# A planner with other costs: PE's durations from the trace, and VectorE kept out of GpSimd's intervals

## The chip, the cores and the metric

The kernel runs on one core of a Trainium2 chip. The metric is the time on the device in microseconds (us). A core has five engines with a queue of instructions each: PE (TensorE, matmuls), DVE (VectorE), ACT (ScalarE), POOL (GpSimd) and SP, which here only issues DMAs. Each engine works its queue in the order in which the program was written, and an instruction whose operands are not ready holds up all that stand behind it. So the time depends on the order in which the instructions of one program are written, also where their set stays the same.

## What is computed

One layer of a hybrid trunk is run for two groups of requests that share the weights: a prompt (16 meta rows and 512 rows) and a sample (64 rows); together 592 rows, of which 576 go on. Cut to its core:

```
h = rms_norm(x, pre_gain)
q,k,v,z,r, sq,sk,sv,sz, mg,ms = split(h @ w_in)        # 2048 -> 11280 columns
log_a = log_sigmoid(r @ w_a2 + b_a) / 16
o_gla = gated linear attention(q, k, v, log_a)         # 4 heads: S = diag(a) S + k v^T, o = q S
y_gla = (rms_norm(o_gla) * silu(z)) @ w_up_gla
o_sb  = stick_breaking_attention(sq, sk, sv)           # 8 heads
y_sb  = (o_sb * silu(sz)) @ w_up_sb
y     = x + rms_norm((sigmoid(mg) * y_gla + sigmoid(ms) * y_sb) @ w_o, post_gain)
```

All data are fp32. Outputs are y, the new keys and values and the GLA state of both groups.

## The kernel before

**Tiles and stages.** Each fp32 product is made of three passes in a reduced format: a weight is split into a high part `whi` (cast by ACT from the raw tile) and the rest `wlo` (raw minus whi, by DVE), the activations likewise into tiles such as `h2h` and `h2l`; PE does hi times hi, hi times lo, lo times hi. A pair of 128-column blocks is multiplied by a Strassen-Winograd scheme: seven products W11, W22, S3, S1, S2, W12, S4 (`ORDERS`), whose weights are the raw quarters or sums of them (`raw<-raw`, DVE). In the projection by w_in each product consists of two units of four k-tiles, 12 matmuls of 288 or 296 columns each, so a pair has 14 units. There are 786 units: 616 in the 44 pairs of the input projection (in order: GLA keys, queries, values and gates; the same for the other heads; the stick-breaking keys, values, queries and gates; the two merge gates), then the up projections, then W_o.

**Streams.** Generators feed the engines: `convert` (ACT, `whi`; it may run four units ahead of PE, since the ring has four buffers), `remain` (DVE, `wlo`), `combine` (DVE, the raw sums), `multiply` (PE). The products' results go through FIFOs (`after`, `follow`): ACT copies a bank to `out` or `u`, and for S2 (`done`, line 488) DVE makes u+bank and u+S1 in place (`u<-u,b`, twice), a sum into `out`, and POOL the last one (`out<-out,u`). A bank that S4 needs comes free only behind the `u` sums, so PE's first unit of S4, two units later, waits for them. A gate's `out` passes through silu (`size`, exp, Ln, subtraction, exp, POOL product; names `e<-out`, `e<-e`, `e<-out,e`, `out<-out,e`) and is then stored. Every store and load is issued on SP's one queue: raw tiles of 512 KB with three buffers, and the tensors that go to DRAM and come back, as d_gk, d_cs.

Beside these runs `background()`: `decays()` (per GLA head two gates, exp, Ln and a scan, written `nu<-reset,tm`, stored to d_cs), then `gla_head` for each of the four heads (`gla_fetch` loads k, cs and q; `gla_level` makes x from cs, exponentiates it on ACT, multiplies by q on DVE and by k on POOL, and PE makes the scores, which DVE copies by a mask, `sc<-lmask,b`), the stick-breaking chains, and the merge.

**What sets the order.** `Plan` writes the program. Each call of an engine goes through `Engine.call`, which tells `Plan.note`; all instructions therefore carry that helper's line, L197 here. `note` gives the instruction a planned start (engine free, operands ready, plus `LATENCY`), and an end by `Plan.cost`. `Plan.run` then resumes the stream whose step is due first:

```
def due(self, e):
    return max(e["ready"] + e["slack"], self.free.get(e["eng"], 0.0)) - self.lead.get(e["name"], 0.0)
```

The planned times reach the chip only as the order on each queue; on the chip an instruction waits for its operands and nothing else. `need` (line 687) also acts on the order alone: a pair's W22 isn't written before the pair two ahead has its first column stored.

Of the kernel before, what the change touches and what calls it, by code (L numbers as in the profile page):

```python
# [9 lines left out]
F32 = mybir.dt.float32  # L10
# [68 lines left out]
class Plan:  # L79


    def __init__(self):
        self.free, self.ready, self.used, self.last, self.streams = {}, {}, {}, 0.0, []
        self.base, self.now = {}, 0.0
        self.quartered, self.psum, self.lead, self.by = set(), set(), {}, {}

    def names(self, x):
# [8 lines left out]
    def at(self, x):  # L96
        return max(self.ready.get(y, 0.0) for y in self.names(x))

    def cost(self, eng, name, out, ins, summed):
        n = 1  # L100
        for x in out.shape[1:]:
            n *= x
        psum = any(x.tensor.name in self.psum for x in ins)
        if eng == "pe":
            dt = ins[0].dtype
            if dt == BF16:
                return 0.107
            if name == "transpose":
                return 0.053 if n < 64 else 0.11
            return max(0.214, n * 1.67e-3) if dt == F32 else max(0.11, n * 0.42e-3) + 0.003  # L110
        if eng == "act":
            return (0.055 if psum else 0.095) + (0.09 if summed or len(ins) > 1 else 0.0) + n * 0.83e-3
        if eng == "dve":
            if name == "tensor_scalar" and not psum:
                return 0.07 + n * 0.52e-3
            return 0.07 + n * (6.3e-3 if name == "reciprocal" else 1.04e-3)
        if name == "memset":
            return 0.04 + n * 0.83e-3
        return 0.15 + n * (3.5e-3 if name == "tensor_scalar" else 2.1e-3)

    def note(self, eng, name, args, kw):
        aps = [x for x in list(args) + list(kw.values()) if isinstance(x, bass.AP)]
        out = kw["out"] if "out" in kw else args[0]
        ins = [x for x in aps if x is not out]
        names = [y for x in ins for y in self.names(x)]
        outs = self.names(out)
        made = outs[1:] or outs
        if "dma" in name:
            size = 4.0
            for x in out.shape:  # L130
                size *= x
            start = max([self.now, self.free.get(eng, 0.0)] + [self.ready.get(x, 0.0) for x in names] + [self.base.get(outs[0], 0.0)])
            self.free[eng] = start + 0.5
            self.free["dma"] = max(self.free.get("dma", 0.0), start + 1.9) + size / 350e3
            end = self.free["dma"] + 1.8
            for x in made:
                self.ready[x] = max(self.ready.get(x, 0.0), end)
            for x in names:
                self.used[x] = max(self.used.get(x, 0.0), end)
            return  # L140
        start = self.free.get(eng, 0.0)
        for x in names + outs:
            by = self.by.get(x)
            if eng != "pe" or by != "pe":
                start = max(start, self.ready.get(x, 0.0) + LATENCY.get((by, eng), 0.1))
        end = start + self.cost(eng, name, out, ins, "accum_out" in kw)
        self.free[eng] = end
        for x in names + outs:
            self.used[x] = max(self.used.get(x, 0.0), end)
        for x in made:  # L150
            self.ready[x] = self.base[x] = end
            self.by[x] = eng
        self.last = end
# [1820 lines left out]
```

## Time and profile before

| | us |
|---|---|
| three runs | 1744.12, 1739.87, 1744.42 |
| their median | 1744.12 |
| the profiled execution, its time | 1741.68 |
| its span, first to last instruction | 1739.9 |
| PE busy | 1670.2 (96% of the span) |
| DVE busy | 1250.6 (72%) |
| ACT busy | 853.8 (49%) |
| POOL busy | 182.2 (10%) |

Matmul times overlap in the pipeline, so PE's busy time is the union of them. Idle time matters where PE has it: the chain that ended last is 89% PE. The views that list what an engine waited for name the instruction that came last before the wait ended. PEclk is TensorE's granted clock as a share of full speed.

### The profile page before, as it was taken

To read this page: it belongs to the slowest core of one execution; us is meant where nothing else is said; L and a number is where in the kernel's file an instruction comes from. 1 tells how busy PE (TensorE), PEld (TensorE's weight loads), DVE (VectorE), ACT (ScalarE), POOL (GpSimd) and SP (SyncE) were. 2 spreads that over 40 slices of the span, in tenths; PEclk is the share of its full clock that TensorE was granted. 3 is DMA by queue.
4 is the path that set the end of the run, shared out by engine and by line. 5 is a ranking of instruction groups with operands and counts; after the bars stand their busy time and mean duration, and the time that the engine had idled before them with its cause. 6 is when DMAs were issued, how large, how long until landed. Compare 5 with 4: busy or idle time off the path is not lost.

```text
span 1739.9 us, 31534 instructions
## 1 busy us (share of the span) xinstructions
PE 1670.2 (96%) x12089; PEld 1610.1 (93%) x12089; DVE 1250.6 (72%) x2081; ACT 853.8 (49%) x1759; POOL 182.2 (10%) x293
## 2 busy tenths in 40 slices
PE   4998999899999999999999999999999999999997
PEld 2798999889999998999999999999999999999996
DVE  5877878887987886886677667666766435687777
ACT  5554444344454353455565555555544323355554
POOL 2100220120130021021020011111000000000000
PEclk9999999999999999999999999999999999999998
DMA  7144234344444424455445544554447444423336
GB/s 189 37 140 131 77 107 139 101 116 123 122 117 128 132 60 119 126 163 159 133 137 152 148 140 117 158 158 126 128 138 218 143 142 124 122 79 103 104 80 218
DMA packets 323904, 224.14 MB, mean 129 GB/s; under 512 B 17436, under 2 KB 293432, under 8 KB 322584
## 3 DMA queue, kind: packets, MB, share of 16 engines
q1 hardware_dynamic: 323016, 219.49, 44.3%
q10 hardware_dynamic: 736, 2.62, 0.4%
q8 instruction: 95, 1.56, 0.4%
q14 instruction: 57, 0.47, 0.1%
HBM read 179.17 MB, written 42.90 MB: 128 GB/s over the span
## 4 chain that ended last, share of the span: by engine, by line
PE 89%; DVE 5%; DMA 2%; ACT 1%; issue 1%; POOL 1%; SPq 0%; DVEq 0%; ACTq 0%; POOLq 0%
PE b L197 89%; DVE wlo L197 2%; DVE raw L197 1%; DMA xt<-in_x_sample 1%; ACT whi L197 0%; DVE u L197 0%; DVE t L197 0%; DMA q<-d_gq 0%; POOL h5l L197 0%; DMA xt<-in_x_prompt 0%; DVE x L197 0%; POOL L L197 0%; DVE out L197 0%; SPq L197 0%; DMA raw<-in_w_in 0%
## 5 line engine op out<-in xcount | busy, mean ns | idle before, releaser
L197 ACT CAST whi<-raw 128x512 fp32r<-128x512 f32 x786 | 482.0, 620 | 627.6 <-PE b L197 516.2
L197 DVE TENSOR_TENSOR wlo<-raw,whi 128x512 fp32r<-128x512 f32 x786 | 552.6, 713 | 303.9 <-ACT whi L197 293.7
L197 DVE TENSOR_TENSOR raw<-raw 128x1024 f32<-128x1024 f32 (+1 forms) x232 | 259.5, 1121 | 6.0
L197 PE MATMUL b<-m,whi 128*128 128x288 f32 x912 | 183.5, 296 | 0.0
L197 PEld LDWEIGHTS b<-m,whi 128*128 128x128 f32 x912 | 146.1, 188 | 0.0
L197 PE MATMUL b<-h0h,whi 128*128 128x288 f32 (+1 forms) x480 | 134.3, 304 | 1.3 <-ACT whi L197 1.3
L197 PE MATMUL b<-m,wlo 128*128 128x288 f32 x456 | 134.2, 294 | 0.0
L197 PE MATMUL b<-h6h,whi 128*128 128x288 f32 (+1 forms) x480 | 133.8, 303 | 0.0
L197 PE MATMUL b<-h6l,whi 128*128 128x288 f32 (+1 forms) x480 | 131.5, 298 | 1.9 <-DVE h6l L197 1.8
L197 PE MATMUL b<-h4h,whi 128*128 128x288 f32 (+1 forms) x480 | 133.0, 302 | 0.0
L197 PE MATMUL b<-h1h,whi 128*128 128x288 f32 (+1 forms) x480 | 132.1, 300 | 0.0
L197 PE MATMUL b<-h0l,whi 128*128 128x288 f32 (+1 forms) x480 | 131.5, 299 | 0.0
L197 PE MATMUL b<-h4l,whi 128*128 128x288 f32 (+1 forms) x480 | 130.4, 296 | 0.0
L197 PE MATMUL b<-h1l,whi 128*128 128x288 f32 (+1 forms) x480 | 130.3, 296 | 0.0
L197 PE MATMUL b<-h0h,wlo 128*128 128x288 f32 (+1 forms) x416 | 124.4, 299 | 1.5 <-DVE wlo L197 1.5
L197 PE MATMUL b<-h4h,wlo 128*128 128x288 f32 (+1 forms) x416 | 123.2, 296 | 1.6 <-DVE wlo L197 1.6
L197 PE MATMUL b<-h1h,wlo 128*128 128x288 f32 (+1 forms) x416 | 123.3, 296 | 0.8 <-DVE wlo L197 0.8
L197 PE MATMUL b<-h6h,wlo 128*128 128x288 f32 (+1 forms) x416 | 123.7, 297 | 0.0
L197 PE MATMUL b<-h2h,whi 128*128 128x288 f32 (+1 forms) x352 | 112.5, 319 | 10.7 <-DVE u L197 10.7
L197 PE MATMUL b<-h2h,wlo 128*128 128x288 f32 (+1 forms) x352 | 107.5, 305 | 1.0 <-DVE wlo L197 1.0
L197 PE MATMUL b<-h5h,whi 128*128 128x288 f32 (+1 forms) x352 | 108.5, 308 | 0.0
L197 PE MATMUL b<-h3h,whi 128*128 128x288 f32 (+1 forms) x352 | 107.9, 307 | 0.0
(263 smaller groups left out, 4084.8 us busy)
## 6 DMA issues: line engine op xcount, KB each, us to landing
raw<-in_w_in SPq DMA_DIRECT2D x176, 512.0 KB, 4.5
raw<-in_w_o SPq DMA_DIRECT2D x32, 512.0 KB, 4.0
raw<-in_w_up_gla SPq DMA_DIRECT2D x16, 512.0 KB, 5.3
raw<-in_w_up_sb SPq DMA_DIRECT2D x16, 512.0 KB, 4.7
d_mg<-out SPq DMA_DIRECT2D x16, 288.0 KB, 2.2
d_ms<-out SPq DMA_DIRECT2D x16, 288.0 KB, 2.1
gate<-d_mg SPq DMA_DIRECT2D x16, 288.0 KB, 5.4
gate<-d_ms SPq DMA_DIRECT2D x16, 288.0 KB, 5.5
```

The costliest lines, as they stand in the source:

```text
L197: return real(*args, **kw)
```

## The change

In `Plan.cost`, five of PE's durations and one of DVE's change: a bf16 matmul is planned with 0.056 us instead of 0.107, a transpose with 0.11 whatever its size, an fp32 matmul with 0.224 at least instead of 0.214, and the reduced-format matmul of 288 columns with 0.1325 us (288 x 0.4167e-3 + 0.0125) instead of 0.124; a `scalar_tensor_tensor` with more than two inputs on DVE with 0.125 instead of 0.07 at its base.

In `Plan.note`, the planned intervals of POOL's operations and of those DVE operations that read two SBUF operands of the output's shape (`shared`: wlo, raw sums, `x<-x,q`, `e<-out,e`, `out<-u,b` where both lie in SBUF, ...) are kept in two lists, and each of either kind is planned to start behind any interval of the other kind that it would overlap. Only planned times change by this, not what is written.

```
+        self.port = {"pool": [], "dve": []}
...
+    def shared(self, out, ins):
+
+        n = [x for x in ins if x.tensor.name not in self.psum and x.shape[1:] == out.shape[1:]]
+        return len(n) > 1
...
-                return 0.107
+                return 0.056
             if name == "transpose":
-                return 0.053 if n < 64 else 0.11
-            return max(0.214, n * 1.67e-3) if dt == F32 else max(0.11, n * 0.42e-3) + 0.003
+                return 0.11
+            return max(0.224, n * 1.67e-3 + 4e-3) if dt == F32 else max(0.112, n * 0.4167e-3 + 0.0125)
...
+            if name == "scalar_tensor_tensor" and len(ins) > 2:
+                return 0.125 + n * 1.04e-3
...
-        end = start + self.cost(eng, name, out, ins, "accum_out" in kw)
+        took = self.cost(eng, name, out, ins, "accum_out" in kw)
+        if name != "memset" and (eng == "pool" or eng == "dve" and self.shared(out, ins)):
+            for t0, t1 in sorted(self.port["pool" if eng == "dve" else "dve"]):
+                if t0 < start + took and t1 > start:
+                    start = t1
+            self.port[eng] = self.port[eng][-23:] + [(start, start + took)]
+        end = start + took
```

Both kernels have the same instructions on every engine (PE 11541, DVE 2073, ACT 1677, SP 640 by the program); their order differs from the first pair on. The changed kernel's helper line is L211. Three places follow in which the order moves.

**DVE around the two `u` sums of S2.** For S2 of pair 18 (pairs counted from 0) before:

```order
L197 TENSOR_TENSOR raw<-raw 128x1024
L197 TENSOR_TENSOR x_6435<-x_6435,q 128x10x32
L197 TENSOR_TENSOR wlo<-raw,whi 128x512 x4
L197 TENSOR_TENSOR raw<-raw 128x1024 x2
L197 TENSOR_TENSOR out<-out,b_6375 128x288
L197 TENSOR_TENSOR u<-u,b_6458 128x288
L197 TENSOR_TENSOR u<-u,b_6418 128x288
L197 TENSOR_TENSOR out<-u,b_6375 128x288
```

For S2 of pair 21 now:

```order
L211 TENSOR_TENSOR raw<-raw 128x1024
L211 TENSOR_TENSOR x_7330<-x_7330,q 128x4x64
L211 TENSOR_TENSOR x_7333<-x_7333,q 128x40x8
L211 TENSOR_TENSOR raw<-raw 128x1024
L211 TENSOR_TENSOR x_7376<-cs 128x20x16 x2
L211 TENSOR_TENSOR u<-u,b_7278 128x296
L211 TENSOR_TENSOR u<-u,b_7228 128x296
L211 TENSOR_TENSOR out<-u,b_7177 128x8
L211 TENSOR_TENSOR out<-u,b_7177 128x288
```

The sums `u<-u,b` stand ahead of the wlo of the third unit behind S2 in both; before, this happens in pairs 4, 8 and 18, now in pairs 10, 16 and 21, and in the places shown six instructions stand between a wlo and the sums now, where three stood before.

**SP, the loads with which the first GLA head starts.** k, cs and q are loaded from DRAM; d_cs is the store of a scan, d_gz that of a gate, raw a weight tile (two loads each). Before:

```order
L197 DMA d_cs_1635<-nu 128x640
L197 DMA lmask<-in_consts 128x512
L197 DMA raw<-in_w_in 128x8x128 x2
L197 DMA k<-d_gk_907 128x528
L197 DMA k<-d_gk_907 128x64
L197 DMA cs<-d_cs_1007 128x640
L197 DMA q<-d_gq_1227 128x512
L197 DMA q<-d_gq_1227 128x64
```

Now:

```order
L211 DMA d_gv_2057<-out 128x592
L211 DMA d_cs_2067<-nu 128x640
L211 DMA lmask<-in_consts 128x512
L211 DMA d_gz_1783<-out 128x576
L211 DMA k<-d_gk_965 128x528
L211 DMA k<-d_gk_965 128x64
L211 DMA cs<-d_cs_1063 128x640
L211 DMA q<-d_gq_1231 128x512
L211 DMA q<-d_gq_1231 128x64
L211 DMA raw<-in_w_in 128x8x128 x8
```

The loads moved from behind two raw loads to behind the gate's store d_gz_1783 (and behind the last scan's d_cs), with eight raw loads now behind them.

**ACT at the end of pair 6 and the start of pair 7, where `whi` of units 92 to 101 stands (a pair has 14 units).** The rows with e are two gates' silu, those with x the head's levels. Before:

```order
L197 ACTIVATE e<-e 128x288
L197 CAST whi<-raw 128x512 x3
L197 ACTIVATE e<-e 128x288
L197 ACTIVATE e<-e,one 128x288
L197 COPY x_2643<-b_2605 128x496
L197 COPY x_2643<-b_2555 128x16
L197 COPY x_2643<-b_2606 128x64
L197 ACTIVATE e<-e 128x288
L197 CAST whi<-raw 128x512 x5
L197 COPY x_2775<-b_2737 128x496
```

Now, where two silu chains and two levels stand ahead of `whi` of unit 98:

```order
L211 CAST whi<-raw 128x512 x2
L211 ACTIVATE e<-e 128x288
L211 ACTIVATE e<-e,one 128x288
L211 ACTIVATE e<-e 128x288
L211 ACTIVATE x_2587<-x_2587 128x640
L211 COPY out<-b_2338 128x8
L211 COPY out<-b_2338 128x288
L211 ACTIVATE e<-e 128x288
L211 ACTIVATE e<-e,one 128x288
L211 ACTIVATE x_2657<-x_2657 128x640
L211 ACTIVATE e<-e 128x288
L211 CAST whi<-raw 128x512 x4
```

The two chains, which stood apart by several `whi` before, now stand in one block with the exponentials of two levels.

## Rows read from the trace of the kernel before

**Rows 1.** The page's head and its first part: busy time of each engine, share of the span, instructions.

```profile
span 1739.9 us, 31534 instructions
PE 1670.2 (96%) x12089; PEld 1610.1 (93%) x12089; DVE 1250.6 (72%) x2081; ACT 853.8 (49%) x1759; POOL 182.2 (10%) x293
```

**Rows 2.** Busy time by stage: the stretch in us from the span's start, its length, then PE, PEld, DVE, ACT, POOL with their instructions, PEclk, DMA share, GB/s. The three stretches are the GLA heads, the stick-breaking chains with the merge gates, and the up and W_o projections.

```profile
50.00:700.00 650.00, 616.76 (x4418) 595.56 (x4417) 520.91 (x863) 307.78 (x615) 97.78 (x133) 0.97 0.39 111
700.00:1340.00 640.00, 637.61 (x4672) 614.99 (x4671) 440.61 (x671) 347.76 (x673) 69.00 (x145) 1.00 0.51 146
1340.00:1739.00 399.00, 390.97 (x2903) 384.72 (x2902) 257.55 (x466) 170.45 (x403) 2.90 (x1) 0.99 0.43 125
```

**Rows 3.** What PE waited for from 50 to 700 us: total us, times, longest.

```profile
PE b L197 <- DVE u L197: 10.7, 3, 4.2
PE b L197 <- DVE cs L197: 5.8, 4, 2.7
PE b L197 <- DMA q<-d_gq: 5.5, 1, 5.5
PE b L197 <- DVE wlo L197: 4.9, 6, 1.6
PE b L197 <- DMA x<-d_gv: 2.7, 2, 1.4
```

**Rows 4.** The same columns as rows 2 for short stretches after a wait (two of seven), and for PE alone in a stretch without waits.

```profile
316.00:326.00 10.00, 5.78 (x30) 5.62 (x29) 8.93 (x17) 2.16 (x5) 2.48 (x4) 0.66 0.49 137
604.00:612.00 8.00, 6.49 (x30) 6.52 (x31) 5.89 (x15) 3.02 (x5) 2.35 (x3) 0.57 0.11 39
...
1500.00:1600.00 100.00, 100.00 (x756) 1.00 0.33 90
```

**Rows 5.** DVE's timeline from 600 us on: start, duration, instruction, count, and idle time before it with its releaser.

```profile
600.94 0.69 DVE L197 TENSOR_TENSOR wlo<-raw,whi 128x512 fp32r<-128x512 f32 x1 [0.91 <-ACT whi L197]
601.67 2.48 DVE L197 TENSOR_TENSOR raw<-raw 128x1024 f32<-128x1024 f32 x2
604.07 0.45 DVE L197 TENSOR_TENSOR out<-out,b 128x288 f32<-128x288 f32 x1
604.43 0.93 DVE L197 TENSOR_TENSOR u<-u,b 128x288 f32<-128x288 f32 x2
```

**Rows 6.** PE's timeline there.

```profile
605.51 0.58 PE L197 MATMUL b<-h2h,whi 128*128 128x288 f32 x1 [3.85 <-DVE u L197]
605.89 0.44 PE L197 MATMUL b<-h2l,whi 128*128 128x288 f32 x1
606.13 0.44 PE L197 MATMUL b<-h2h,wlo 128*128 128x288 f32 x1
```

**Rows 7.** SP's timeline at the first head's loads.

```profile
163.21 1.33 SPq L197 DMA_DIRECT2D k<-d_gk  x2
165.00 0.32 SPq L197 DMA_DIRECT2D cs<-d_cs  x1
165.42 0.84 SPq L197 DMA_DIRECT2D q<-d_gq  x2
```

**Rows 8.** PE's timeline there.

```profile
170.65 1.62 PE L197 MATMUL b<-q,k 128*128 128x128 f32 x6 [5.54 <-DMA q<-d_gq]
```

**Rows 9.** DVE's timeline around 455 us, where x of a head's level is made from cs.

```profile
452.88 0.52 DVE L197 TENSOR_TENSOR out<-out,b 128x8 f32<-128x8 f32 x2
455.52 0.89 DVE L197 TENSOR_TENSOR x<-cs 128x320 f32<-128x320 f32 x2 [2.12 <-DMA d_og<-x]
```

**Rows 10.** DVE's groups of instructions of one shape: count, busy us, mean ns of one, idle time before them and what ended it.

```profile
L197 DVE TENSOR_TENSOR wlo<-raw,whi 128x512 fp32r<-128x512 f32 x786 | 552.6, 713 | 303.9 <-ACT whi L197 293.7 <-PE b L197 3.8 <-DMA raw<-in_w_in 0.9
L197 DVE TENSOR_TENSOR raw<-raw 128x1024 f32<-128x1024 f32 x176 | 221.5, 1258 | 4.9
L197 DVE TENSOR_TENSOR x<-cs 128x320 f32<-128x320 f32 x48 | 22.6, 513 | 10.0 <-DMA d_og<-x 7.4 <-DMA cs<-d_cs 2.6
L197 DVE COPY_PREDICATED sc<-lmask,b 128x320 f32<-128x320 int32 x24 | 15.2, 632 | 0.8 <-DVE sc L197 0.5
L197 DVE SCALAR_TENSOR_TENSOR e<-out 128x288 f32<-128x288 f32 x32 | 14.3, 448 | 1.4 <-POOL out L197 1.4
L197 DVE TENSOR_TENSOR_SCAN nu<-reset,tm 128x640 f32<-128x640 f32 x4 | 5.9, 1483 | 0.0
```

**Rows 11.** The same for ACT.

```profile
L197 ACT CAST whi<-raw 128x512 fp32r<-128x512 f32 x786 | 482.0, 620 | 627.6 <-PE b L197 516.2 <-DVE raw L197 80.1 <-issue 10.4
L197 ACT ACTIVATE e<-e 128x288 f32<-128x288 f32 x64 | 28.5, 445 | 44.9 <-DVE e L197 44.5
L197 ACT ACTIVATE x<-x 128x640 f32<-128x640 f32 x28 | 20.5, 737 | 25.4 <-DVE x L197 25.3
L197 ACT ACTIVATE e<-e,one 128x288 f32<-128x288 f32 x32 | 17.2, 537 | 1.0
```

**Rows 12.** DVE's timeline at 197 us.

```profile
197.38 1.35 DVE L197 TENSOR_TENSOR wlo<-raw,whi 128x512 fp32r<-128x512 f32 x1
198.65 0.48 DVE L197 TENSOR_TENSOR x<-x,q 128x320 f32<-128x320 f32 x1
```

**Rows 13.** POOL's timeline there.

```profile
196.75 1.43 POOL L197 TENSOR_TENSOR x<-x,k 128x320 f32<-128x320 f32 x1 [1.66 <-ACT x L197]
```

**Rows 14.** Of the DMA issues, the loads of stick-breaking queries: KB each, median us from issue to landing.

```profile
q<-d_sq SPq DMA_DIRECT2D x8, 256.0 KB, 2.9
```

## The prediction

> **What bounds the kernel now.** I read the busy times first: PE works in 1670.2 of 1739.9 us, the other engines far less [rows 1]. So a new order can only give or take PE's idle time and the time it works at a lower clock. By stage that time lies almost all in the first 700 us: from 50 to 700 PE is busy for 616.8 of 650 us at a mean clock of 0.97; in the next 640 us 2.4 us are idle, and behind 1340 us 8.0, part of it the tail [rows 2]. The list of PE's waits for 50 to 700 us names what ended them: the `u` sums 10.7 us in three waits, cs 5.8, the load of q 5.5, wlo 4.9, the loads of v 2.7 [rows 3].
>
> Then the clock. Where PE works without a wait, 756 matmuls take 100 us, 132.3 ns each, so a unit of 12 takes 1.59 us, at full clock (2.4 GHz) [rows 4]. Behind the wait at 605.5 us matmuls follow each other after 0.24 us [rows 6]: the lower level, 1.2 GHz. The clock of 604 to 612 is 0.57 in the mean [rows 4]: 6.8 of these 8 us at the half (0.57 x 8 = 6.8 x 0.5 + 1.2). PE waited in the first 1.1 of them, so 5.7 us ran at half speed and lost 2.85. Six waits behind 80 us (all those of 2.6 us and more) have such a stretch, waits up to 1.6 us have none; worked out alike they lose 1.45 to 2.85, in sum 12.4, some 2.07 each. PE's idle time from 80 to 700 us, summed from its timeline, is 27.4. So 39.8 us are at stake before; that all went is the most that an order could give.
>
> **How a wait arises.** Three of before's waits show the rule by which I price the new ones. `whi` of unit k waits for a ring buffer that PE frees with unit k-4, and wlo of k for whi. At 605 us: PE had nothing left at 601.66 (605.51 - 3.85). DVE's wlo at 600.94 was the last of the units converted ahead; behind it stood two raw sums (2.48), an `out` sum (0.45) and the two `u` sums (0.93), done at 605.36; PE began 0.15 later [rows 5, 6]. With the end of the unit before S4 as zero, wlo is done 1.5 to 1.65 later, then come DVE's block and some 0.25 to PE, less what PE has of background work. This gives 4.04, 3.6 and 2.8 for the three waits; measured are 3.85, 4.2 and 2.6.
>
> For a block in front of the wlo of any unit the cover is larger: PE has four converted units, 6.35 us, beside background; the last wlo is done at 1.65. A block up to about 6.35 - 1.65 - 0.69 - 0.25 = 3.8 us (its own wlo of 0.69 counted) costs nothing, a longer one its excess.
>
> **The change part by part.** The costs in `cost` and the intervals in `note` do nothing on the chip by themselves. Planned PE time for a unit of 288 columns rises by 12 x 0.0085 = 0.10 us to 1.59, which is the measured pace [rows 4]. The rest is order, stretch by stretch:
>
> 1. The `u` sums. Before, they stand behind the critical wlo in pairs 4, 8, 18: 10.7 us. Now in pairs 10, 16, 21. In pair 21 the block is two raw sums 2.48, two `x<-x,q` at 0.48 [rows 12], two `x<-cs` at 0.45 [rows 9], two `u` 0.93: 5.3 us; with 1.65 and 0.25, less 2.2 of PE's background, 5.0. Pairs 10 and 16 in the same way 5.15 and 4.55. Sum 14.7. One wlo less far behind, without background, are pairs 15 and 17: 1.2 and 1.5. Together 17.4, from 10.7 (as before) to 22.
> 2. The start of the first head. Before, q was issued at 165.42 and PE began at 170.65, after 5.5 us [rows 7, 8]. Now the loads stand behind d_gz_1783, which waits for a whole silu chain that stands behind the scan. From PE's end of unit 71: wlo at 1.65; on DVE an `out` sum 0.6, `e<-out,e` 0.45, the sum ahead of the scan 0.8 (an estimate for 640 columns from 0.45 for 288 and 0.74 on ACT for 640), the scan 1.5, `e<-out` 0.45 [rows 10]: 5.45; exp and Ln 0.98 [rows 11] with two hand-offs: 6.6; `e<-out,e` 7.2, exp 7.8, POOL's product 8.8, the store's issue 9.2; then k 1.3, cs 0.4 and q 0.8 of issue [rows 7]: q is issued from 10.9 to 11.75. A load of that size lands after 2.9 us for the stick-breaking queries [rows 14], after 5.2 here before, with raw loads ahead of it. I take the shorter, since no raw load stands ahead: 14.4. PE comes there at 6.35. The wait is 8.0 (5.5 to 9.7).
> 3. The start of pair 7, unit 98. DVE has 20 instructions between the wlo of 97 and 98: three `out` and two `u` sums of 0.45 and three pieces of 8 columns at 0.16, four silu steps at 0.45, three masked copies at 0.51 to 0.63 [rows 10], four `x<-cs` and one `x<-x,q`: 8.6 us, against a cover of 3.8. Behind the last silu step ACT's exp (0.45) and the cast of 98 (0.62) [rows 11] still come, as ACT's order shows: 1.65 + 8.6 + 0.45 + 0.62 + 0.69 + 0.7 of hand-offs = 12.7; PE is there at 6.35 and some background, 6.7. The wait is 6.0 (3 to 6.5).
> 4. Unit 104: ACT has two silu chains' steps, two exps of 640 columns at 0.74 and two copies ahead of its whi, with POOL's product between: 2.5 (0 to 4.5). Unit 184: the product q,s needs a chain of state sums that DVE has four units late: 2.6 (0 to 3). Unit 300: 13 DVE instructions, 7.6 us, the last of them `x<-cs` behind a d_og store, for which DVE waited 2.1 before [rows 9]: 5.1 (3 to 5.5).
> 5. What goes: the cs copies now stand level with PE's need, so 5.8 us go; the loads of v, 2.7; before's wait for wlo, 4.9, is replaced by the blocks above.
> 6. The stages behind 700 us: sums and copies move by a unit or two, with 0.7 us or more to spare where PE reads them; 0, within 1 either way. The start to 80 us: 0 to -0.5.
>
> Idle: 17.4 + 8.0 + 6.0 + 2.5 + 2.6 + 5.1 = 41.6. Seven of these waits are of 2.6 us or about that and more: 7 x 2.07 = 14.5 of clock. 56.1 against 39.8 is +16.3. On the profiled execution's 1741.68 (1.8 outside its span, 2.4 below the median of the runs) this makes 1758.
>
> Bounds: with the `u` sums as before, the head's start as before and nothing in 3 and 4: 16.2 + 4 x 2.07 = 24.5, or -15: 1726. With all upper ends, 22 + 9.7 + 6.5 + 4.5 + 3 + 5.5 = 51 and 7 x 2.85 = 20: +31, 1773.
>
> **VectorE and GpSimd.** A wlo that starts during POOL's `x<-x,k` (196.75 to 198.18) takes 1.35 us [rows 12, 13]; undisturbed ones take 0.69 [rows 5]; the mean of all is 0.713, so stretching costs 786 x 0.023 = 18 us of DVE's time [rows 10]. But DVE idles 293.7 us for whi alone [rows 10], and the chain waits on DVE in few places. So I count nothing for it.
>
> The Trainium skill says on the page "SBUF — State Buffer", section "SBUF: two separate sides", that a VectorE operation with two SBUF inputs and a GpSimd operation that reads SBUF take one port pair as an exclusive lock, so that the later one blocks for the whole of the other. The rows agree with that: 1.35 is POOL's remaining 0.8 and some 0.55 of work. By that rule, planning the two apart returns DVE's 18 us where they would meet; PE gains only what of it ended a wait, which is the third rival.
>
> **Rivals.**
> - The blocks in 3 and 4 do not come last and the waits for cs, v and wlo go: faster, 1726, the lower bound. It decides where a block ends before PE has used its four units, that is below 3.8 us. For it: PE's planned pace is now the measured one, so work is planned where PE really is. Against: the order's blocks of 8.6 and 7.6 us. Chance 0.16.
> - The new waits come at about half, since one that delays PE gives DVE the time to catch up: idle 29, clock 10: 39, 1741 to 1747, the same. Chance 0.14.
> - The collisions of DVE and POOL lie on the chain: those in blocks that PE waits for (a raw sum or `x<-x,q` taking 1.7 to 2.6 instead of 1.24) go, some 1 us in each of six waits, with the order otherwise as counted in the first rival: 1720. Chance 0.04. The cited page stands behind this one.
> - Worse: d_gz's wait on SP also holds the raw loads behind it, and late loads cost PE one more wait of 5 us and its clock: 1758 + 5 + 2 to 1773 and above. Chance 0.08.
>
> **How the numbers follow.** Forecast 0.58, rivals as given. A measurement of this kernel can tell 0.3%, 5.2 us: faster is below 1738.9, slower above 1749.4. Faster takes the first and third rival, 0.20, less a little that ends within: 0.18. The same takes 0.14 and the low edge of the forecast: 0.16. Slower 0.66. The likeliest case has its own range of 1748 to 1773; the range for 8 in 10 reaches down into the faster cases: 1734 to 1773.
>
> **What would show it.** In the changed kernel's waits of PE: `u` three long waits of 4.5 to 5.2 us in pairs 10, 16 and 21; one wait of 8 us for q's load at about unit 76; one of 6 us for whi or wlo at unit 98, and one of 5 at unit 300; cs gone from the list; seven stretches of low clock. Wrong would be: fewer than four waits above 2.6 us between 80 and 700 us, or any of 2 us and more behind 700.

## The result, and the profile after

The changed kernel takes 1760.89 us (median of five runs, 1758.74 to 1763.43); the kernel before takes 1742.20 (five runs, 1739.87 to 1744.42). The ratio is 1.0111, with a 95% interval of 1.0094 to 1.0128: 18.7 us slower. Forecast were 1758 us, in a range of 1734 to 1773, with 0.66 for slower. One execution of all, one of e1's six, was disturbed as a whole (2389.51 us) and is left out of the times and ratios below.

The page's head and its first part, which answer to [rows 1]:

```profile
span 1760.8 us, 31518 instructions
PE 1677.0 (95%) x12089; PEld 1615.8 (92%) x12089; DVE 1252.7 (71%) x2081; ACT 854.9 (49%) x1759; POOL 183.2 (10%) x293
```

All engines have the same work to within 7 us; PE's busy time is 6.8 us longer and the span 20.9. By stage, with the columns of [rows 2]:

```profile
50.00:700.00 650.00, 605.32 (x4298) 584.43 (x4296) 510.80 (x831) 304.46 (x606) 90.75 (x124) 0.96 0.39 110
700.00:1340.00 640.00, 639.81 (x4674) 616.64 (x4675) 446.17 (x695) 345.22 (x676) 78.14 (x155) 0.99 0.49 139
1340.00:1760.00 420.00, 410.56 (x3029) 402.02 (x3027) 266.66 (x480) 179.38 (x416) 2.90 (x1) 0.99 0.44 131
```

From 50 to 700 us PE is busy for 605.3 us where it was for 616.8; the middle stage is as before. What PE waited for from 50 to 700 us, as in [rows 3] (total us, times, longest):

```profile
PE b L211 <- DVE x L211: 17.4, 9, 4.1
PE b L211 <- DMA q<-d_gq: 7.8, 1, 7.8
PE b L211 <- DVE wlo L211: 6.9, 5, 4.0
PE b L211 <- ACT whi L211: 6.3, 4, 3.2
PE b L211 <- DVE s L211: 1.3, 1, 1.3
PE b L211 <- DMA x<-d_gv: 1.2, 1, 1.2
PE b L211 <- POOL x L211: 1.1, 1, 1.1
PE b L211 <- DVE u L211: 0.8, 1, 0.8
```

cs is off the list, as forecast, and the loads of v are down to one wait. The load of q, wlo and whi have grown. The `u` sums, which were to be the largest entry, are down to 0.8 us; x, which had 1.3 us before, has 17.4. Behind 700 us PE has one wait longer than 2 us, 2.3 for diag, an operand of the last products, where it had 1.2 before. By the prediction's own list, a wait of 2 us and more there was to be a sign that it is wrong.

Summed from PE's timeline, the waits of 0.3 us and more between 80 and 700 us are 39.6 us, before 28.6 (sums of waits below are made in the same way). In that stretch the clock is at its lower level eight times, for 51.2 us in all, before six times for 34.1; half of PE's busy time in them is lost: 21.1 us, before 12.4. That is 11.0 + 8.7 = 19.7 of the span's 20.9 us. The rest is a sum of small differences: the first units start 2.6 us later than in the trace of before, the waits at unit 617 and in the tail are 2.5 us more, the waits for POOL in the middle stage 1.0 less; what takes back the remaining 2.9 was not followed up.

**Place by place.** The units are counted from the kernel's first; each wait is read from PE's timeline.

| unit | forecast us | measured us | ended by |
|---|---|---|---|
| 76, first head | 8.0 | 7.8 | load of q |
| 98 | 6.0 | 1.4 + 3.2 | x, whi |
| 104 | 2.5 | 1.1 + 1.1 + 1.2 | POOL's x, whi, load of v |
| 152, pair 10 | 5.15 | 0.9 + 3.0 | x |
| 236, pair 16 | 4.55 | 0.6 + 4.05 | x |
| 306, pair 21 | 5.0 | 4.1 | x |
| 222 and 250 | 1.2 and 1.5 | 0.7 and 0.8 | whi, `u` |
| 184 | 2.6 | 1.3 | state sums |
| 300 | 5.1 | 4.0 | wlo |
| 156, 240 | none | 1.6 + 1.5 | x |

Forecast were 41.6 us; the same places measure 35.3, and four others that were not forecast 4.3 (units 156 and 240, and two of 0.5 and 0.65).

**The first head.** SP's timeline, which answers to [rows 7]:

```profile
199.65 0.34 SPq L211 DMA_DIRECT2D d_cs<-nu  x1
200.09 0.38 SPq L211 DMA_DIRECT2D lmask<-in_consts  x1
202.89 0.32 SPq L211 DMA_DIRECT2D d_gz<-out  x1
203.26 0.92 SPq L211 DMA_DIRECT2D k<-d_gk  x2
204.22 0.43 SPq L211 DMA_DIRECT2D cs<-d_cs  x1
204.75 0.85 SPq L211 DMA_DIRECT2D q<-d_gq  x2
```

PE's timeline there, which answers to [rows 8]:

```profile
208.56 2.05 PE L211 MATMUL b<-q,k 128*128 128x128 f32 x8 [7.80 <-DMA q<-d_gq]
```

d_gz is issued at 202.89, the moment the gate's product is there, 2.4 us behind the end of lmask's issue; only then come k, cs and q. Counted from PE's end of unit 71, at 194.4, that is 8.5, where the working had 9.2, and PE begins at 14.2, where it had 14.4.

**Pair 10.** DVE's timeline, which answers to [rows 5]:

```profile
373.78 0.68 DVE L211 TENSOR_TENSOR wlo<-raw,whi 128x512 fp32r<-128x512 f32 x1
374.50 1.22 DVE L211 TENSOR_TENSOR raw<-raw 128x1024 f32<-128x1024 f32 x1
375.64 1.15 DVE L211 TENSOR_TENSOR x<-x,q 128x320 f32<-128x320 f32 x1
376.71 1.21 DVE L211 TENSOR_TENSOR raw<-raw 128x1024 f32<-128x1024 f32 x1
377.85 0.94 DVE L211 TENSOR_TENSOR u<-u,b 128x296 f32<-128x296 f32 x2
```

PE's timeline, which answers to [rows 6]:

```profile
376.94 2.37 PE L211 MATMUL b<-x 128*128 128x64 f32 x10 [3.04 <-DVE x L211]
379.06 0.59 PE L211 MATMUL b<-h2h,whi 128*128 128x296 f32 x1
```

The block is as the working had it: behind the wlo at 373.78 come two raw sums, an `x<-x,q` and the `u` sums, done at 378.79. But PE has another instruction in front of S4: the background product b<-x, which takes the x that DVE finished at 376.79. PE waits for it, works on it for 2.1 us at the low clock, and starts S4 at 379.06, 0.3 us behind the `u` sums. Both end within 0.3 us, so the profile names the first of two waits for one block.

### The profile page after: what moved, and what is told of

It is laid out like the page before. It is cut to its first block, busy times and chain, and to the rows that moved or that the text cites. A ratio compares the mean times of both kernels' runs of the same rounds, so it can differ in the third digit from the quotient of the medians.

```text
span 1760.8 us, 31518 instructions
## 1 busy us (share of the span) xinstructions
PE 1677.0 (95%) x12089; PEld 1615.8 (92%) x12089; DVE 1252.7 (71%) x2081; ACT 854.9 (49%) x1759; POOL 183.2 (10%) x293
## 4 chain that ended last, share of the span: by engine, by line
PE 88%; DVE 4%; DMA 3%; issue 2%; ACT 2%; POOL 1%; SPq 0%; ACTq 0%; DVEq 0%; POOLq 0%
PE b L211 88%; DMA xt<-in_x_sample 1%; DVE wlo L211 1%; DVE x L211 1%; DMA d_og<-x 1%; ACT whi L211 0%; DVE raw L211 0%; DMA stage<-d_og 0%; SPq L211 0%; POOL h5l L211 0%; DMA xt<-in_x_prompt 0%; ACT e L211 0%; DVE t L211 0%; DVE out L211 0%; DMA q<-d_gq 0%
## 5 line engine op out<-in xcount | busy, mean ns | idle before, releaser
L211 ACT CAST whi<-raw 128x512 fp32r<-128x512 f32 x786 | 483.5, 620 | 645.8 <-PE b L211 538.7
L211 DVE TENSOR_TENSOR wlo<-raw,whi 128x512 fp32r<-128x512 f32 x786 | 549.4, 709 | 293.3 <-ACT whi L211 280.6
L211 DVE TENSOR_TENSOR raw<-raw 128x1024 f32<-128x1024 f32 (+1 forms) x232 | 259.7, 1121 | 5.6
L211 PE MATMUL b<-m,whi 128*128 128x288 f32 x912 | 183.5, 296 | 0.0
L211 PEld LDWEIGHTS b<-m,whi 128*128 128x128 f32 x912 | 146.0, 188 | 0.0
L211 PE MATMUL b<-h0h,whi 128*128 128x288 f32 (+1 forms) x480 | 134.6, 305 | 4.5 <-ACT whi L211 4.5
L211 PE MATMUL b<-h6l,whi 128*128 128x288 f32 (+1 forms) x480 | 131.9, 299 | 3.2 <-DVE h6l L211 1.8
L211 PE MATMUL b<-m,wlo 128*128 128x288 f32 x456 | 134.3, 294 | 0.0
L211 PE MATMUL b<-h4h,whi 128*128 128x288 f32 (+1 forms) x480 | 134.1, 304 | 0.0
L211 PE MATMUL b<-h6h,whi 128*128 128x288 f32 (+1 forms) x480 | 133.5, 303 | 0.0
L211 PE MATMUL b<-h1h,whi 128*128 128x288 f32 (+1 forms) x480 | 133.3, 302 | 0.0
L211 PE MATMUL b<-h0l,whi 128*128 128x288 f32 (+1 forms) x480 | 131.7, 299 | 0.0
L211 PE MATMUL b<-h4l,whi 128*128 128x288 f32 (+1 forms) x480 | 130.5, 296 | 0.0
L211 PE MATMUL b<-h1l,whi 128*128 128x288 f32 (+1 forms) x480 | 130.5, 296 | 0.0
L211 PE MATMUL b<-h0h,wlo 128*128 128x288 f32 (+1 forms) x416 | 124.8, 300 | 1.6 <-DVE wlo L211 1.5
L211 PE MATMUL b<-h6h,wlo 128*128 128x288 f32 (+1 forms) x416 | 124.1, 298 | 0.0
L211 PE MATMUL b<-h4h,wlo 128*128 128x288 f32 (+1 forms) x416 | 123.2, 296 | 0.7 <-DVE wlo L211 0.7
L211 PE MATMUL b<-h1h,wlo 128*128 128x288 f32 (+1 forms) x416 | 123.1, 296 | 0.0
L211 PE MATMUL b<-h2h,whi 128*128 128x288 f32 (+1 forms) x352 | 109.6, 311 | 1.5 <-DVE u L211 0.8
L211 PE MATMUL b<-h3h,wlo 128*128 128x288 f32 (+1 forms) x352 | 105.4, 299 | 4.2 <-DVE wlo L211 4.2
L211 PE MATMUL b<-h3h,whi 128*128 128x288 f32 (+1 forms) x352 | 108.0, 307 | 1.1 <-ACT whi L211 1.1
L211 PE MATMUL b<-h5h,whi 128*128 128x288 f32 (+1 forms) x352 | 107.9, 306 | 0.0
```

What stands on the lines that cost most here:

```text
L211: return real(*args, **kw)
```

## The experiments

**Which part of the change.** e1 takes the intervals away and keeps the new costs:

```
-        if name != "memset" and (eng == "pool" or eng == "dve" and self.shared(out, ins)):
+        if False:
```

> The changed kernel without the intervals (the planner's new costs alone). Theory, the lost time comes from the intervals: in this order no u sum stands three units behind S2 or later, and the longest block in front of a wlo is 4.7 us instead of 8.6; PE's waits from 80 to 700 us sum to 15 to 20 us (the start of the first head about 5.5, unit 190 about 2, cs and v about 2.5 each) with three or four stretches of low clock: about 1726 us (1718 to 1735), faster than both kernels. Rival, the slower planned PE makes the bad order: 1755 to 1762 us, with the long waits at the units of the changed kernel.

1731.25 us (median of five), ratio to the kernel before 0.9931 (0.9910 to 0.9951): faster than both kernels. Its waits of PE from 50 to 700 us:

```profile
PE b L211 <- DVE x L211: 5.2, 6, 1.4
PE b L211 <- DVE wlo L211: 4.0, 5, 1.5
PE b L211 <- DMA x<-d_gv: 3.8, 2, 2.2
PE b L211 <- DMA q<-d_gq: 3.4, 1, 3.4
PE b L211 <- ACT whi L211: 2.7, 2, 1.4
PE b L211 <- DVE cs L211: 1.9, 1, 1.9
```

No wait is longer than 3.4 us; between 80 and 700 us they sum to 17.8, with three stretches of low clock, which lose 6.6.

e2 is the kernel before with the intervals and its old costs:

```
+        if name != "memset" and (eng == "pool" or eng == "dve" and self.shared(out, ins)):
+            for t0, t1 in sorted(self.port["pool" if eng == "dve" else "dve"]):
...
             if dt == BF16:
                 return 0.107
```

> The kernel before with the intervals alone (the planner's old costs). Theory, the intervals make the bad order: u sums stand late in four pairs and blocks of 5 to 8.5 us in front of the wlo of units 76, 86, 104, 142, 160, 212 and 300; waits from 80 to 700 us of about 40 us and eight or nine stretches of low clock: about 1765 us (1755 to 1785). Rival, the costs make it: 1740 to 1746 us, as before.

1786.39 us, ratio 1.0256 (1.0237 to 1.0274): 43 us slower than the kernel before, a little beyond the expected range. Its waits:

```profile
PE b L209 <- DVE x L209: 23.1, 6, 7.2
PE b L209 <- DMA q<-d_gq: 9.7, 1, 9.7
PE b L209 <- ACT whi L209: 6.2, 5, 3.2
PE b L209 <- POOL x L209: 5.3, 3, 2.5
PE b L209 <- DVE u L209: 3.3, 2, 2.3
PE b L209 <- DMA x<-d_gv: 2.8, 3, 1.3
```

The waits between 80 and 700 us sum to 52.3, where about 40 were expected, and the low clock loses 24.6 more. Both are 35.9 us more than before; from 700 to 1340 us there are 6 us more of waits (8.5, before 2.2) and a stretch of low clock that loses 1.7. So the two parts pull in opposite directions: the costs alone bring about 12 us, the intervals alone cost 43, and both together cost 18.7.

e7 and e8 keep the new costs and one half of the rule: in e7 only DVE's operations are planned behind POOL's intervals, in e8 only POOL's behind DVE's:

```
-                if t0 < start + took and t1 > start:
+                if eng == "dve" and t0 < start + took and t1 > start:
```

> The change with one half of the interval rule: only DVE's operations are planned behind POOL's intervals. Theory, each half makes the plan late and the order worse: the first head starts at unit 76 with a wait of about 8 us, a u sum stands three units late in pair 5, blocks of 6.6 to 7.5 us in front of the wlo of units 86, 160 and 356; waits of some 36 us, 1750 to 1760 us. Rival, only the other half is to blame: 1729 to 1736 us, as without the intervals.

1761.39 us, ratio 1.0109 (1.0083 to 1.0134), with waits of 33.4 us between 80 and 700 and 17.9 lost by the clock. A little above the range; the first head starts at unit 76 with a wait of 8.3 us, as expected.

> The change with the other half: only POOL's operations are planned behind DVE's intervals. Theory, as above: the first head starts early with a wait of about 5 us, u sums stand three units late in pairs 14 and 18, blocks of 6 to 7 us in front of the wlo of units 76, 86, 212 and 268; waits of some 30 us, 1744 to 1753 us. Rival, only DVE's half is to blame: 1729 to 1736 us.

1752.71 us, ratio 1.0048 (1.0030 to 1.0067), waits of 31.3 and 16.5 by the clock. Either half makes the order worse than without the rule; neither rival holds.

e10 and e11 ask whether this hangs on one choice of the planner's other constants. e10 is e1, and e11 the changed kernel, each with:

```
-SLACK = 0.4
+SLACK = 0.3
-LEADS = {'convert': -0.2, 'remain': 0.4, 'combine': 0.4, 'multiply': -0.1, 'queue': 0, 'slower': 0}
+LEADS = {'convert': -0.2, 'remain': 0.4, 'combine': 0.4, 'multiply': -0.1, 'queue': 0, 'slower': 0.2}
```

> As e1 (new costs, no intervals), with SLACK 0.3 instead of 0.4 and a lead of 0.2 for silu's line. Theory, a time follows from the waits that stand in the order: one u sum stands two units late without background (pair 6), one long block of 7.6 us in front of the wlo of unit 188, other blocks 4.2 us and less: waits from 80 to 700 us of 12 to 16 us, 1720 to 1732 us, faster than before and not slower than e1. Rival, e1's gain is one lucky order, and small changes of the constants lose it: 1735 to 1745 us.

1731.79 us, ratio 0.9940 (0.9924 to 0.9957): within 1 us of e1's time, with another order. Between 80 and 700 us its waits are 20.3, where 12 to 16 were expected, and the clock loses 11.2: 7.1 us more than in e1. Ahead of 80 and behind 700 us it loses 8 less (waits 2.7 less in the start and 2.8 less from 700 to 1340 us, and 2.5 less of low clock).

> As e10, with the intervals. Theory, the intervals make a worse order whatever the constants: u sums three units late in pairs 9 and 15, blocks of 5.7 to 7.7 us in front of the wlo of units 76, 142, 226 and 300; waits of some 28 to 34 us and five or more stretches of low clock: 15 to 25 us slower than e10, 1740 to 1752 us. Rival, with other constants the intervals do no harm: within 5 us of e10.

1740.65 us, ratio 0.9988 (0.9975 to 1.0001), 8.9 us slower than e10 and no different from the kernel before. The sign holds; the size is about a third of the 30 us between the changed kernel and e1, and below the expected 15 to 25. The waits are 24.3 us, where 28 to 34 were expected, with four stretches of low clock. How much the rule costs depends on the order that happens to come out.

**Which wait is whose.** For the next kernels the order is written out: the planner's choices of one kernel, one letter for each, stand in a string, and `run` takes the stream that is named next.

```
-            e = min(able, key=self.due)
+            i = "0123456789abcdefghijklmnop".index(STEPS[self.step])
+            self.step += 1
+            e = [x for x in able if x["id"] == i]
+            e = e[0]
```

Without further edit this writes the same program. Letters are then moved, and what moves in the program is given with each.

e4 moves SP's loads:

```
 DMA lmask<-in_consts 128x512
-DMA d_gz<-out 128x576
 DMA k<-d_gk 128x528
...
 DMA q<-d_gq 128x64
+DMA d_gz<-out 128x576
```

PE, DVE and ACT keep their order; on POOL the gate's product moves behind four `memset`s of the head's tiles.

> The changed kernel's order, written out, with the five loads of k, cs and q on SP ahead of the gate's store d_gz instead of behind it; the order of PE, DVE and ACT is unchanged. Theory, the store's wait for silu delays the loads: they are issued 2.5 to 3.5 us earlier, and PE's wait of 7.8 us at unit 76 falls to about 4.5 (3.8 to 5.2). Rival, the store of the scan to d_cs and the landing set the end: the wait stays at 7 to 8 us.

One run: 1758.53 us, and PE's wait at unit 76 is 6.05 us, from 7.8. SP's timeline in e4:

```profile
196.46 0.34 SPq L292 DMA_DIRECT2D d_cs<-nu  x1
198.87 0.85 SPq L292 DMA_DIRECT2D q<-d_gq  x2
199.82 0.38 SPq L292 DMA_DIRECT2D d_gz<-out  x1
```

PE's timeline there:

```profile
203.61 1.62 PE L292 MATMUL b<-q,k 128*128 128x128 f32 x6 [6.05 <-DMA q<-d_gq]
```

q is issued 2.4 us behind d_cs where it was issued 5.1 behind it: the loads are 2.7 us earlier, as expected. But from q's issue to PE's start it takes 4.7 us, in the changed kernel 3.8. So the wait lost 1.75 of the 2.7; it lies between what the two theories expected.

e3 moves two things in pairs 10, 16 and 21 (two sums `out<-u,b` go with the `u` sums); for pair 10, on DVE and on PE:

```
 TENSOR_TENSOR wlo<-raw,whi 128x512
+TENSOR_TENSOR u<-u,b 128x296
+TENSOR_TENSOR u<-u,b 128x296
 TENSOR_TENSOR x<-x,q 128x160x2
...
 TENSOR_TENSOR raw<-raw 128x1024
-TENSOR_TENSOR u<-u,b 128x296
-TENSOR_TENSOR u<-u,b 128x296

-MATMUL b<-x 128x64 x5
 MATMUL b<-h2h,whi 128x296
...
 MATMUL b<-h2h,wlo 128x296
+MATMUL b<-x 128x64 x5
```

> The changed kernel's order, written out, with two moves in pairs 10, 16 and 21: DVE's u sums stand ahead of the wlo of the second unit behind S4's first, and PE's background product b<-x behind S4's first unit. Theory, these two hold PE there, each as late as the other: the waits of 3.9, 4.6 and 4.1 us at units 152, 236 and 306 fall to 1.5 or less each, and with their clock the time falls by 8 to 15 us, to about 1749. Rival, PE would run into the next wlo at once: the waits only move by a unit, and the time stays within 3 us of 1760.9.

1757.09 us, 3.8 less than the changed kernel; the waits became 2.3 + 1.4 in pair 10, 0.6 + 3.8 one unit later in pair 16, and 4.9 in pair 21. All waits between 80 and 700 us are 38.3, from 39.6, and the clock loses 17.6, from 21.1. The rival was nearer.

e5 makes the same move of the `u` sums in the kernel before, where the profile named them, in pairs 4, 8 and 18; for pair 8:

```
-TENSOR_TENSOR wlo<-raw,whi 128x512 x4
-TENSOR_TENSOR raw<-raw 128x1024 x2
+TENSOR_TENSOR wlo<-raw,whi 128x512 x2
 TENSOR_TENSOR u<-u,b 128x296
...
+TENSOR_TENSOR wlo<-raw,whi 128x512 x2
+TENSOR_TENSOR raw<-raw 128x1024 x2
```

> The kernel before, its order written out, with one move in pairs 4, 8 and 18: S2's u sums stand on DVE ahead of the wlo of the second unit behind S4's first (behind it, and behind two raw sums, before). Theory of the prediction, the place of the u sums alone makes these three waits: 10.7 us of waits and 6.3 us of low clock go, less up to 4 for waits that take their place: 1726 to 1731 us. Rival, the raw sums hold up the next wlo all the same, and the wait only moves by a unit or two: 1739 to 1744 us.

1743.40 us (ten runs), ratio 1.0007 (0.9994 to 1.0020): nothing. Its waits from 190 to 700 us:

```profile
PE b L278 <- DVE x L278: 11.1, 6, 4.9
PE b L278 <- DVE cs L278: 5.4, 2, 2.7
PE b L278 <- DVE wlo L278: 3.4, 5, 1.6
PE b L278 <- DMA x<-d_gv: 2.9, 2, 1.5
PE b L278 <- DVE u L278: 0.5, 1, 0.5
```

`u` is down from 10.7 to 0.5 us, and x is up from 1.3 to 11.1. The waits are at the same three places, up to four units later and with the other name; they sum to 11.2 us in both kernels. The rival held.

e6 takes whi of units 98 to 100 ahead of the silu block on ACT:

```
 ACTIVATE x<-x 128x640
+CAST whi<-raw 128x512 x3
 COPY out<-b 128x8
...
 ACTIVATE e<-e 128x288
-CAST whi<-raw 128x512 x4
+CAST whi<-raw 128x512
```

> The changed kernel's order, written out, with whi of units 98 to 100 on ACT ahead of the block of silu steps and exponentials, and wlo of 98 and 99 on DVE behind nine of the block's instructions instead of all twenty. Theory, the block holds PE at unit 98: the wait for whi of 3.2 us goes, the one of 1.4 us for x ahead of it stays; about 5 us less with the clock, near 1756. Rival, the silu steps that are pushed back make the next wait longer (d_gz, k of unit 104): the sum of the waits at units 98 to 105 stays at 8 us.

One run: 1755.88 us. Its waits from 248 to 280 us:

```profile
PE b L292 <- POOL x L292: 3.3, 2, 2.6
PE b L292 <- DVE x L292: 2.6, 1, 2.6
PE b L292 <- ACT whi L292: 1.1, 1, 1.1
PE b L292 <- DMA x<-d_gv: 1.0, 1, 1.0
```

The wait for whi of 3.2 us is gone, and waits for x of 2.6 us ahead of unit 98 and 2.6 ahead of 99 have come; the sum over units 98 to 105 is 8.0 us in both. The rival held for the waits. The time is the one that the theory named, but not for its reason: the start is 2 us shorter, and the clock loses 17.3 us in place of 21.1, mainly since no stretch of low clock follows the wait at unit 184, which the move leaves as it was.

e9 moves the GLA head's levels as a whole, on every engine, three units later in the three pairs, and the `u` sums ahead as in e3; on PE in pair 10:

```
-MATMUL b<-x 128x64 x5
-MATMUL b<-x 128x64 x5
 MATMUL b<-h2h,whi 128x296
...
 MATMUL b<-h0h,wlo 128x288
+MATMUL b<-x 64x64 x4
+MATMUL b<-x 128x64 x5
+MATMUL b<-x 128x64 x5
```

> The changed kernel's order, written out, with the u sums ahead as in e3, and in pairs 10, 16 and 21 all steps of the GLA head's levels (x from cs, the exponentials, the products with q and k, PE's b<-x and the masked copies) some three units later on every engine. Theory, PE's queue holds b<-x earlier than DVE can have its x in that stretch, and three units of 1.6 us are enough: the waits of 15.9 us in seven places at units 152, 156, 236, 240 and 306 fall to 4 or less, with their clock some 15 to 19 us less: 1742 to 1747 us. Rival, DVE has too much to do there: waits of the same sum come back within eight units, 1754 to 1760 us.

1774.07 us, ratio 1.0175 (1.0159 to 1.0192): worse than the changed kernel by 13 us. At unit 152 only 1.2 us are left, but 3.3 + 1.5 came at 155, 1.3 at 159 and 2.0 at 160; the other two pairs likewise. In all three, 15.9 us of waits became 23. The rival held, and more than it said came back.

e12 moves in pair 10 alone: the `u` sums as in e3, and of the levels only PE's products (with what follows them in that head), so that x has three units' time before its product:

```
-MATMUL b<-x 128x64 x5
-MATMUL b<-x 128x64 x5
 MATMUL b<-h2h,whi 128x296
...
 MATMUL b<-h0h,wlo 128x288
+MATMUL b<-x 128x64 x5
+MATMUL b<-x 128x64 x5
 MATMUL b<-h0h,whi 128x288
```

> The changed kernel's order, written out, with a move in pair 10 alone: the u sums ahead as in e3, x of the two levels where it stands on DVE, and only PE's products b<-x of these levels, with all that follows them in this head, three units later (e9 had moved x and its product together). Theory, PE waits there because a product stands in its queue right behind the place where DVE writes its x, with no unit in between: with three units between them the waits of 0.9 and 3.0 us at unit 152 go, and those from unit 150 to 165 (5.6 us in the changed kernel, 9.3 in e9) fall to 2.5 or less. Rival, DVE's block is too long for that stretch, wherever the products stand: they stay at 5 or more.

One run: 1760.87 us. Its waits from 368 to 412 us:

```profile
PE b L292 <- DVE x L292: 3.2, 1, 3.2
PE b L292 <- DVE wlo L292: 2.5, 2, 2.3
PE b L292 <- ACT whi L292: 0.7, 1, 0.7
PE b L292 <- DVE u L292: 0.5, 1, 0.5
```

At unit 152 0.5 us is left, as the theory said, and the two products run without a wait. Then PE waits 2.3 us for the wlo of unit 158 and 3.2 us for the next level's x at 159. Together 6.0 from unit 150 to 165, against 5.6 in the changed kernel: the rival held for the sum.

Five moves of single things (e3, e5, e6, e9, e12) took the named wait away, and in each the sum of that stretch came back within a few units. DVE's busy time shows what the places have in common; columns as in [rows 2], of the changed kernel:

```profile
364.00:379.00 15.00, 11.07 (x81) 10.68 (x81) 14.71 (x24) 6.45 (x14) 5.76 (x6) 0.90 0.34 95
```

In the 15 us up to the `u` sums of pair 10, DVE is busy for 14.7 and PE for 11.1; in pair 16 DVE has 14.3 (537 to 552 us), in pair 21 13.1 (687 to 702). In the kernel before it has 13.9 in pair 4 (188 to 203 us), but 10.6 in pair 8 (305 to 320) and 11.4 in pair 18 (590 to 605): there it stood idle earlier in the stretch, and what is common is only the last part, in which it works without a gap, for 4.4 us in pair 18 [rows 5] and for 9.6 in pair 8. Nor does a full DVE alone make a long wait: in e1 it is busy for 14.4 of the 15 us from 365, and PE's two waits there are 1.6 us for a load and 1.9 for cs. So I read it as DVE being behind with all of a block, and who comes first in the block decides only the name of PE's wait; the moves that left the sum as it was show the second half of this, the first is argued. That DVE's work, together with the chain of a level (x, exponential, product, PE, masked copy), also sets the waits that came back in e9 and e12 is how I read them; it was not taken apart further.

## Why the prediction was right, and where not

**Right by its own steps.** The sum of the places, 41.6 us of waits, met 39.6 in the same stretch, and every place of it has a wait of PE in the trace. The first head's chain was right to 0.7 us at the store and to 0.2 where PE begins. cs and the loads of v went as said, and the stages behind 700 us moved by the 1 to 2.5 us of their own small waits, which is more than the 1 us allowed for; among them is the wait of 2.3 us for diag, one of its two signs of being wrong. That wait costs 1.1 us more than before, so the sign was set too fine for what it was to show.

**The clock's term was too small.** Forecast were 7 x 2.07 = 14.5 us, measured 21.1, in eight stretches, 2.6 us each, which last up to 10.2 us where before's lasted 6.8 at most. The price by the length of the wait, none up to 1.6 us and 2.07 from 2.6 on, did not hold either: two of the eight follow the waits of 1.6 us at unit 156 and of 1.3 at unit 184. Nor does one wait have one price. That of 1.3 us at unit 184 stands in six traces; in the changed kernel's and those of e3 and e4 a stretch of 6.8 us at the lower level (1.2 GHz) follows it, in those of e6, e9 and e12 none. The waits came 2.0 us below the forecast and the clock 6.6 above it: 56.1 forecast, 60.7 measured. That these two errors offset each other in part is luck.

**The step that failed** is that the `u` sums are the cause in pairs 10, 16 and 21, and with them in before's pairs 4, 8 and 18. The block was right and its length nearly (14.7 us of waits forecast in the three pairs, 12.7 measured), so the time was. But e5 takes the `u` sums out of before's blocks and gains nothing, and in the changed kernel x ends PE's wait 2 us ahead of them. What counts, as far as these moves show, is DVE's block as a whole, not the sum that stands last in it. Pricing each place by its block worked for that reason; an edit that follows the name of the wait does not.

**The rivals.** That blocks are absorbed (1726) did not come; nor did the half-size waits, nor a wait for raw loads behind d_gz: the list of waits has none. The third, that DVE and POOL no longer meet, can be read directly; the last line is POOL's:

```profile
L211 DVE TENSOR_TENSOR wlo<-raw,whi 128x512 fp32r<-128x512 f32 x786 | 549.4, 709 | 293.3 <-ACT whi L211 280.6 <-PE b L211 6.3
L211 DVE TENSOR_TENSOR x<-x,q 128x320 f32<-128x320 f32 x24 | 17.7, 738 | 0.0
374.76 1.68 POOL L211 TENSOR_TENSOR x<-x,k 128x320 f32<-128x320 f32 x1 [2.66 <-ACT x L211]
```

The mean wlo takes 709 ns, from 713 [rows 10], and `x<-x,q` 738, from 651. At 375.64 above, one of them takes 1.15 us beside the POOL product that ran from 374.76 to 376.44, where an undisturbed one takes 0.48 [rows 12]. The plan keeps them apart in its own times, and on the chip they meet about as before: DVE's busy time is 1252.7 us, from 1250.6. Even in e2, where it is 1245.1, the 5.5 us gained there stand against 43 lost to waits.

By the Trainium skill's "SBUF — State Buffer", section "SBUF: two separate sides", the operation that starts second is blocked for the whole of the other. The 1.15 us agree nearly: 0.80 until POOL's end, and 0.35 behind it, somewhat less than a whole 0.48. So the rule is near the truth here, and still a worse order follows from planning by it.

**What was left of the cause.** e1 and e2 show that the intervals lose the time and the costs gain some. In all three pairs of kernels that differ by the rule alone (43, 30 and 8.9 us), and with either half of it, the rule is slower; that it must be so for other orders is not shown. Why the planner comes to a worse order with them was not measured. In its code `due` chooses a stream without the interval, and `note` moves the start afterwards; and a DVE instruction that is planned to wait for POOL holds all of DVE's plan. That these are the reason is argued, not shown.

## What to carry to other kernels

A planner's model can be made truer and its order worse: judge each part of such a change alone, since here costs taken from the trace brought 12 us and a true rule on a shared port cost more than that. Price a new order by the blocks that stand in front of what the bounding engine needs, and count the lower clock, but not as a fixed price of a wait, since the same wait had it in three traces and not in three others. Do not move single instructions because a wait bears their name, when the engine that is waited for has worked without a gap up to the wait's end: look at that whole block first.

## What the runs showed of the hardware

Loads issued 2.7 us earlier released PE only 1.75 earlier: right behind lmask's load, and with a store behind them, q took 4.7 us from its issue to PE's start, where 3.8 were enough when they came later (e4). The scan `nu<-reset,tm`, 1.48 us in the trace of before [rows 10], took 2.08 once in the changed kernel, where it started at 197.55 beside a POOL product of 0.81 us that ran from 197.47; the other three there took 1.48. This single case suggests that POOL lengthens the scan, too. And the first product with a wlo starts at 62.9 us in the trace of before, at 65.5 in the changed kernel's, and between 61.9 and 64.7 in those of e3, e4, e6, e9 and e12, whose order up to there is the changed kernel's: two profiles of one order can differ by 3.6 us in the start alone. The clock differs in the same way: behind the wait of 1.3 us at unit 184 the mean granted clock of 443 to 451 us is 0.59 in the changed kernel's trace and 1.00 in e6's.
